# Spreading the gates of a product-key expert layer: one comparison of four tokens against a number row in PSUM

## The chip, the cores and the metric

The kernel runs on one core of a Trainium2 chip. The metric is the device time of one execution in microseconds (us). Five engines matter: TensorE (PE in the profile, its weight loads PEld), VectorE (DVE), ScalarE (ACT), GpSimd (POOL) and SyncE (SP), which here only starts transfers. SBUF is the working memory, PSUM the memory that TensorE writes its products to; each has 128 partitions.

## The reference

Two transformer blocks over 512 tokens of width 1024, in fp32. The first block mixes its tokens by attention and a delta rule, and then passes them through PEER, a layer of 16384 experts with one neuron each. Only PEER's gates are touched here. The second block ends in another expert layer. PEER, cut to what matters:

```
q = x @ w_query                                   # 8 heads, 256 wide
s1, s2 = q[..., :128] @ keys1.T, q[..., 128:] @ keys2.T   # 128 scores each
v1, i1 = top_k(s1, 16);  v2, i2 = top_k(s2, 16)
cand = v1[:, None] + v2[None, :]                  # 256 pairs
top_s, top_p = top_k(cand, 16)
e_idx = i1[top_p // 16] * 128 + i2[top_p % 16]
gate = softmax(top_s)
y = sum over the 8 * 16 chosen: gate * gelu(x . u[e_idx]) * v[e_idx]
```

## The kernel before

Function `peer` computes PEER for the first 384 tokens (ND) without gathering: each meets all 16384 experts, 128 expert tiles of 128, and the gates are zero where an expert wasn't chosen. For the last 128 tokens the chosen rows of u and v are gathered one by one. The steps stand in this order in the code:

- The query projection and the top 16 of each head (`topk`), for all four tiles of 128 tokens.
- `select(tt)`, for each tile of tokens: it turns the places of the chosen pairs into two key numbers, by comparing with a short number row (L1119), multiplying by the key numbers (L1122, on DVE for the first two tiles, on POOL for the others) and adding up (L1123). For the first three tiles the two key numbers and the gate of each choice are transposed and stored as `selT`, with the choices on the partitions and the tokens along the row; `negT` holds two of them negated.
- `spread(tt)`, for the first three tiles: it lays the gates out by expert. A token's 128 gates over i1 and i2 form a 128x128 matrix, the product of two one-hot matrices over the choices: `ohb`, 1 where i2 equals the column's number, and `oha`, the gate where i1 equals it. Four tokens are a group, 32 groups a tile, 96 in all. For each group `onehots` makes `oha` and `ohb`, `product` multiplies them (four matmuls into one PSUM bank, L1169; in fp32 each shows as two passes), `store` copies the bank out (L1175), and every fourth group sends 1 MB of gate columns to DRAM by SP. In program order a group's one-hots stand beside the product of the group before and the store of the one before that. The one-hots have four buffers.
- The 128 columns' numbers 0 to 127 (`k_iota`) lie in SBUF. `MIX` says by tile and parity of the group how a group's four gated one-hots are made: one or none by ACT with two activations (L1160, L1161), one or none by DVE alone in one instruction (L1158), and the other two to four by a comparison on DVE (L1146) that POOL then multiplies by the gates (L1154). `ohb` is one comparison of 512 elements on DVE (L1146).
- `first(et)`, for the first 28 expert tiles, is independent of the gates: the tile of u is split in two parts by ACT and POOL (L170, L171), 24 matmuls give its products with the tokens (L165 to L167, tile `ups`), and ACT takes the gelu (L1007). PE works on these between the products of the spreading.
- After that the expert stage: for each group of eight expert tiles the gates come back from DRAM and are multiplied in (L1275), and v is multiplied in (L165 to L167, tile `vacc`; results added to the residual by L1343), with the remaining `first` tiles and the gathered rows in between.

A planner that walks the program with estimated costs orders the instructions of each engine; dependencies between engines are kept by semaphores, and each engine takes its instructions in that order.

Of the kernel before, what the change touches and what calls it, by code (L numbers as in the profile page):

```python
# [9 lines left out]
F32 = mybir.dt.float32  # L10
# [30 lines left out]
def shape_consts():  # L41
    """Constants that depend on shapes alone."""
# [6 lines left out]
    # attention: distance and log of the number of patterns holding the offset  # L49
# [5 lines left out]
    # delta rule masks: two chunks of 64 on the partitions  # L55
# [31 lines left out]
def layout(I):  # L87
    """Data layout only: transposes, reshapes, concatenation."""
# [49 lines left out]
class K:  # L138
# [34 lines left out]
    def tables(s, after, name="natural_log_exp_and_others"):  # L173
        """one set of tables for what follows an activation, here both of log and exp"""
        with s.tc.issue_after(after.ins):
            s.nc.scalar.preload_act_table_set(name)

    def rsqrt(s, out, x, eps):
        """out = (x + eps) ** -0.5"""
        s.nc.scalar.activation(out, x, AF.Ln, bias=eps)  # L180
        s.nc.scalar.activation(out, out, AF.Exp, scale=-0.5)

    def rsqrt6(s, out, x, tmp, eps=1e-6, bias=None):
        """out = (x + eps) ** -0.5, with a step of Newton's method"""
# [6 lines left out]
    # ---------------------------------------------------------------- modulation  # L191
# [9 lines left out]
    def ada_parts(s, which, wname, bname, rep, lo, n, sel, wp, pp, tags=("mm", "tr"), spaces=None):  # L201
        """mod columns of the n column blocks (512 wide) from lo on, a block to each next(), two row tiles to a load.
        Block q goes to row q of each quarter, a quarter for every fourth row tile; its other rows get zeros."""
# [23 lines left out]
    # ------------------------------------------------- normalised, modulated input  # L227
    def rms(s, xT, wp, pp, tag="mm", ps=None):
        """rsqrt(mean(x*x) + eps)"""
# [12 lines left out]
    def modnorm(s, xT, r, gname, which, part, hhi, hlo, wp, keep=None):  # L242
        """h = x * r * (g * (1 + scale)) + shift, split in two parts."""
# [13 lines left out]
    def proj_tile(s, wsrc, hhi, hlo, wp, pp, eng=None, n=KT, tag="mm"):  # L257
        """One 128-column tile of the first n row tiles of h @ w, columns on partitions; returns the PSUM tile."""
# [11 lines left out]
    def out_proj(s, wname, mhi, mlo, xT, gatecol, wp, pp, ms=None, ahead=None, begun=0):  # L270
        """x += gate * (mix @ w) from tile begun on; the mean of its squares into ms; loads that run ahead of what follows"""
# [20 lines left out]
class Banks:  # L292
    """PSUM banks by tag"""
# [7 lines left out]
def block1(s, alloc, after):  # L301
    nc, tc, A = s.nc, s.tc, s.A
    mm = nc.tensor.matmul
    with ExitStack() as c1:
# [13 lines left out]
        with ExitStack() as c2:  # L318
# [6 lines left out]
            def room():  # L325
                """pools of what runs beside the recurrence"""
# [16 lines left out]
            def tail(forward):  # L343
                """the output projection of all but the last pair beside the last of the recurrence"""
# [24 lines left out]
            with ExitStack() as c3:  # L369
# [13 lines left out]
                # token shift coefficient of the token itself  # L383
# [3 lines left out]
                for ct in [24, 25, 16, 12, 17, 18, 19, 13, 14, 15, 20, 21, 22, 23]:  # L387
# [9 lines left out]
                    if 4 <= j < 8:  # L397
                        # kk: normalised by head
# [45 lines left out]
            # the last pair  # L444
# [23 lines left out]
ATT = 4, 3, 3, 3     # steps of the attention to each filling  # L468
ADA = ((2, 0, 1, 1), (1, 1, 1, 1), (1, 1, 1, 0), (2, 1, 0, 0), (1, 2, 2, 2))    # parts of the modulation to each filling
OUT = 1, 2, 2, 3, 0  # tiles of the output projection to each filling  # L470


def attention(s, P, ap, qkd, vd, mixd):
    """softmax over the three patterns at once, two heads and 128 queries at a time; a step to each next()"""
# [45 lines left out]
def rwkv(s, c, P, zrd, mixd, kkd, sad, gd, room, fill, tail):  # L520
    """Both directions of the delta rule in chunks of 64 steps; the second runs on reversed time.
    Goes on with every next(): constants, gates, the first pair's decays, and the rest, which yields the last
    pair's part of the mix.

    Partitions hold two heads' features (e, f) or two chunks' steps (c, t).  A product that keeps
    the two apart contracts over all 128 partitions, one operand being zero outside its own half.
    """
# [8 lines left out]
    class Room:  # L536
        """a tile in the pool of its tag"""
# [6 lines left out]
    if True:  # L544
        flip = kp.tile([128, 128], F32, name="k_flip")
        # these in places that are needed later
# [8 lines left out]
        ka1 = kp.tile([128, 4], F32, name="ka1")       # 1 - k_a  # L555
# [3 lines left out]
        hwa = kp.tile([128, 16], F32, name="hwa")       # half of w0, a0  # L559
        nc.vector.tensor_scalar(hwa, s.v("w0", 0, 16), 0.5, None, OP.mult)  # L560
        # blocks outside the written ones stay zero
# [22 lines left out]
        def sigmoids(j, dr):  # L584
            """of the decay and of a, 0.5 + 0.5 tanh(x / 2)"""
# [31 lines left out]
        def elementwise(h, dr):  # L617
            """decayed r, kk, b, k of one direction, the last two without their decay"""
# [29 lines left out]
        def by_head(ar, cum, x, y):  # L648
            """b~, k~ of either head"""
# [7 lines left out]
        def within(h, dr, ar, bd, x, y):  # L657
            """products within the chunks"""
            QQ, U, yacc = h.QQ, h.U, h.y
            # token-major  # L660
# [11 lines left out]
            ta = wp.tile([128, 4, 2, 2, 64], F32, name="ta", bufs=3)      # head, (alpha, A_ak v)  # L672
            ps = transposed(ar[:, 0, :])
            nc.scalar.activation(ta[:, :, :, 0, :], ps.rearrange("p a (e f) -> p a e f", e=2), AF.Copy)
            tb = wp.tile([128, 4, 2, 2, 64], F32, name="tb", bufs=3)      # head, (A_rb, b~)
# [5 lines left out]
            # within-chunk products [s, t]  # L681
            db = wp.tile([128, 8, 64], F32, name="db", bufs=1)
            E = wp.tile([128, 8, 64], F32, name="E", bufs=3)
            for t2 in range(2):
                pv = P.tile([128, 2, 2, 2, 64], F32, name="pvy", tag="mm")       # (A_ak v | k~ v y)
                pq = P.tile([128, 2, 2, 64], F32, name="pq", tag="mm")
                for ti in range(2):
                    tt = 2 * t2 + ti
                    pa = P.tile([128, 2, 2, 2, 64], F32, name="pa", tag="mm")     # (b~, k~), head, (alpha, r)
# [27 lines left out]
            # diagonal blocks of 16, one on each lane  # L717
# [8 lines left out]
        def solve(j, dr, held, zd, xd, QQ, PB, RP, y):  # L726
            """(I - A_ab)^-1 and what follows from it"""
            ar, ta, tb, E = held
            Z, V, W = Zb[dr], Vb[dr], Wb[dr]
            # inverses of the blocks of 16, and their transposes for the first three of a chunk  # L730
# [8 lines left out]
            # blocks of 32 from blocks of 16  # L739
# [641 lines left out]
def block2_mix(s, xT, begin_moe, ms=None, pu=None):  # L1381
    nc, tc, A = s.nc, s.tc, s.A
    mm = nc.tensor.matmul
    with ExitStack() as c0:
# [16 lines left out]
        with ExitStack() as c1:  # L1401
# [24 lines left out]
            with ExitStack() as c2:  # L1426
# [122 lines left out]
                def c64(x):  # L1549
                    return x.rearrange("p (c t) -> p c t", t=CH)  # L1550
# [620 lines left out]
```

## Time and profile before

| | |
|---|---|
| median of 3 runs | 2857.38 us |
| lowest and highest | 2854.79 and 2861.47 us |
| span of the profiled execution, first to last instruction | 2856.4 us |
| busy share of the span: PE, DVE, ACT, POOL | 91%, 70%, 37%, 41% |
| selection and spreading | from about 866 to 1145 us |
| busy in it, 893 to 1145: PE, DVE, ACT, POOL | 190, 249, 142, 165 us |

The profile gives no time of its own for its execution beside the span; the median of the runs lies 1.0 us above that. The busy shares of the whole mix stages with different limits, so the stretch of the edit has to be read by itself. Durations of successive instructions on DVE and ACT overlap a little in the trace, so that sums of durations exceed the busy time.

### The profile page before, as it was taken

Reading aid. Unit: us, or ns where it says so; the run is one execution under the profiler, and the core shown is the slowest. Engines: PE = TensorE matmul, PEld = TensorE weight load, DVE = VectorE, ACT = ScalarE, POOL = GpSimd, SP = SyncE. Lnnn points to the kernel's source line nnn. Section 1 sums busy time; section 2 is a strip of 40 time slices with the busy share of each in tenths; the row PEclk is TensorE's granted clock in tenths of the full one; section 3 lists DMA queues with packets and bytes.
Section 4 is the critical chain, followed back from the end, with each engine's and each line's share of the span. In section 5 each row is a group of like instructions: output and inputs, shape, how many; then the busy total and the mean of one; then the engine's idle time right before and its main releaser. Section 6 shows DMA issues by size and latency. Waiting matters only on the chain. (4 is left out here: it accounts for less than half of the span.)

```text
span 2856.4 us, 44680 instructions
## 1 busy us (share of the span) xinstructions
PE 2586.5 (91%) x16918; PEld 2042.6 (72%) x16918; DVE 1999.3 (70%) x3833; ACT 1059.1 (37%) x1946; POOL 1159.9 (41%) x860
## 2 busy tenths in 40 slices
PE   7999888987996786899999999999998999989995
PEld 4764456645886775889999999999986665654442
DVE  3666567544899999788888887878865467563323
ACT  3344434422434465333333333333333353231121
POOL 0012212121534666887776776776542223200002
PEclk9999999998998899999999999999999999889998
DMA  6528763451312465788888888887672222069984
GB/s 243 176 80 273 214 195 87 146 166 58 106 60 76 124 178 166 275 313 312 304 285 282 290 295 286 299 294 270 208 239 96 80 64 79 4 261 413 414 350 170
DMA packets 257160, 587.84 MB, mean 206 GB/s; under 512 B 48024, under 2 KB 120240, under 8 KB 246448
## 3 DMA queue, kind: packets, MB, share of 16 engines
q1 hardware_dynamic: 201856, 393.71, 40.2%
q0 software_dynamic: 38016, 138.43, 14.2%
q10 hardware_dynamic: 17072, 52.83, 5.0%
q8 instruction: 134, 2.20, 0.3%
q14 instruction: 82, 0.67, 0.1%
HBM read 529.05 MB, written 55.84 MB: 205 GB/s over the span
## 5 line engine op out<-in xcount | busy, mean ns | idle before, releaser
L165 PE MATMUL vacc<-gh,vhi 128*128 128x384 f32 x1024 | 346.6, 339 | 19.3 <-DVE xres L1343 13.9
L165 PE MATMUL ups<-phhi,uhi 128*128 128x384 f32 x1024 | 348.8, 341 | 10.4 <-ACT ge L1007 10.4
L167 PE MATMUL ups<-phhi,ulo 128*128 128x384 f32 x1024 | 348.3, 340 | 5.9 <-POOL ulo L171 4.3
L166 PE MATMUL ups<-phlo,uhi 128*128 128x384 f32 x1024 | 348.2, 340 | 1.0 <-DVE phlo L253 1.0
L166 PE MATMUL vacc<-gl,vhi 128*128 128x384 f32 x1024 | 344.8, 337 | 0.7 <-DVE gl L171 0.7
L167 PE MATMUL vacc<-gh,vlo 128*128 128x384 f32 x1024 | 325.6, 339 | 11.2 <-POOL vlo L171 10.2
L170 ACT ACTIVATE vhi<-vraw 128x512 fp32r<-128x512 f32 x256 | 160.2, 631 | 325.1 <-PE vacc L166 130.7
L170 ACT ACTIVATE uhi<-uraw 128x1024 fp32r<-128x1024 f32 x128 | 135.7, 1060 | 302.1 <-PE ups L166 258.7
L1227 DVE CUSTOM_DVE_ANT_0 row<-row,phtok 128x1024 f32<-128x1024 f32 x128 | 203.7, 1594 | 34.2 <-DMA row<-u_rows,peid 28.0
L171 POOL TENSOR_TENSOR vlo<-vraw,vhi 128x512 fp32r<-128x512 f32 x128 | 193.5, 1512 | 78.3 <-ACT vhi L170 71.4
L165 PEld LDWEIGHTS vacc<-gh,vhi 128*128 128x128 f32 x1024 | 194.1, 190 | 25.1 <-DVE xres L1343 18.0
L1232 DVE SCALAR_TENSOR_TENSOR acc<-row,dot,acc 128x1024 f32<-128x1024 f32 x127 | 192.4, 1515 | 19.5 <-DMA row<-peer_v,peid 19.4
L1218 POOL DMA_INDIRECT row<-peer_v,peid x128 | 170.5, 1332 | 86.0 <-DVE acc L1232 36.6
L165 PEld LDWEIGHTS ups<-phhi,uhi 128*128 128x128 f32 x1024 | 196.2, 192 | 10.9 <-ACT ge L1007 10.7
L167 PEld LDWEIGHTS vacc<-gh,vlo 128*128 128x128 f32 x1024 | 191.6, 190 | 15.8 <-POOL vlo L171 12.8
L167 PEld LDWEIGHTS ups<-phhi,ulo 128*128 128x128 f32 x1024 | 195.9, 191 | 7.7 <-POOL ulo L171 5.5
L166 PEld LDWEIGHTS ups<-phlo,uhi 128*128 128x128 f32 x1024 | 196.1, 192 | 1.5 <-DVE phlo L253 1.3
L166 PEld LDWEIGHTS vacc<-gl,vhi 128*128 128x128 f32 x1024 | 194.2, 190 | 1.4 <-DVE gl L171 1.2
L1275 POOL TENSOR_TENSOR ge<-ge,wg 128x384 f32<-128x384 f32 x124 | 162.5, 1319 | 75.2 <-DMA wg<-wdr 60.0
L1218 POOL DMA_INDIRECT row<-u_rows,peid x128 | 171.4, 1339 | 52.5 <-DVE dot L1227 20.5
L171 DVE TENSOR_TENSOR ulo<-uraw,uhi 128x1024 fp32r<-128x1024 f32 x100 | 141.8, 1418 | 45.6 <-ACT uhi L170 45.0
L171 DVE TENSOR_TENSOR vlo<-vraw,vhi 128x512 fp32r<-128x512 f32 x128 | 129.4, 1011 | 52.5 <-ACT vhi L170 50.3
(658 smaller groups left out, 5840.4 us busy)
## 6 DMA issues: line engine op xcount, KB each, us to landing
uraw<-peer_u SPq DMA_DIRECT2D x128, 512.0 KB
vraw<-peer_v SPq DMA_DIRECT2D x256, 256.0 KB
wgu<-w_gu SPq DMA_DIRECT2D x32, 2048.0 KB
adaw<-ada_w SPq DMA_DIRECT2D x96, 512.0 KB
wdn<-w_dn SPq DMA_DIRECT2D x32, 1024.0 KB
wd<-wst SPq DMA_DIRECT2D x20, 1024.0 KB
wg<-wd ACTq DMA_DIRECT2D x16, 1280.0 KB
wraw<-w_in SPq DMA_DIRECT2D x22, 512.0 KB
```

The costliest lines, as they stand in the source:

```text
L165: mm(ps, lhsT=L[0], rhs=R[0], start=first, stop=False)
L166: mm(ps, lhsT=L[0], rhs=R[1], start=False, stop=False)
L167: mm(ps, lhsT=L[1], rhs=R[0], start=False, stop=last)
L170: s.nc.scalar.activation(hi, x, AF.Copy)
L171: return (eng or s.nc.vector).tensor_tensor(lo, x, hi.bitcast(F32), OP.subtract)
L1218: nc.gpsimd.indirect_dma_start(out=r, out_offset=None, in_=(urows, vrows)[which], in_offset=bass.IndirectOffsetOnAxis(ap=eid[:, p:p + 1], ...
L1227: nc.vector.tensor_tensor_reduce(out=r, in0=r, in1=htok, scale=1.0, scalar=0.0, op0=OP.mult, op1=OP.add, accum_out=dot[:, p:p + 1])
L1232: nc.vector.scalar_tensor_tensor(acc, r, dot[:, p:p + 1], acc, OP.mult, OP.add)
L1275: i = (nc.vector if grp == 0 and e % 2 == 0 else nc.gpsimd).tensor_tensor(g3, g3, W[0][:, :, e, :], OP.mult)
```

## The change

It concerns the gated one-hots and the number row. The number row is copied once by ACT into a PSUM bank of its own, and every comparison in `select` and `spread` reads it from there; the bank comes from the transposed tiles (tag `tr`), which go from three buffers to two. The two one-hots of a group become one tile, `oht`, filled by one comparison of 2 x 4 x 128 elements on DVE. The gates are multiplied in afterwards, in place: for two of the four tokens by one POOL instruction, for the other two by one ACT copy each with the gate as scale. `MIX`, `negT` and its activations go. In `select`, the multiply of the second tile of tokens moves from DVE to POOL. The rest of the diff removes comments.

```
-            pp1 = c1.enter_context(tc.tile_pool(name="pq", bufs=3, space=PSUM))
...
+            P = Banks(c1, tc, "pq", mm=3, tr=2, io=1)
...
-            iota = s.const("iota128", kp)
+            iota0 = s.const("iota128", kp)
+            iota = P.tile([128, 128], F32, name="iotap", tag="io")
+            nc.scalar.activation(iota, iota0, AF.Copy)
...
-                    (nc.vector if tt < 2 else nc.gpsimd).tensor_tensor(oh4, oh4, xf[:, :, None, :].to_broadcast([128, 8, 16, 16]), OP.mult)
+                    (nc.gpsimd if tt else nc.vector).tensor_tensor(oh4, oh4, xf[:, :, None, :].to_broadcast([128, 8, 16, 16]), OP.mult)
...
-                nc.scalar.activation(negT[:, :, 128 * tt:128 * tt + 128], ps[:, 0:3:2, :], AF.Copy, scale=-1.0)
...
-                    a = wp.tile([128, 4, 128], F32, name="oha", bufs=4)
-                    b = wp.tile([128, 4, 128], F32, name="ohb", bufs=4)
-                    na, nd = MIX[tt][g % 2]
-                    n = 4 - na - nd                                 # by DVE and Pool; then by DVE alone; then by ACT
-                    if n:
-                        equal(a, 0, n)
-                        nc.gpsimd.tensor_tensor(a[:, 0:n, :], a[:, 0:n, :], selT[:, 2, t0:t0 + n, None].to_broadcast([128, n, 128]), OP.mult)
-                    for i in range(n, 4):
-                        at = slice(t0 + i, t0 + i + 1)
-                        if i < n + nd:
-                            nc.vector.scalar_tensor_tensor(a[:, i, :], iota, selT[:, 0, at], selT[:, 2, at].to_broadcast([128, 128]), OP.is_equal, OP.mult)
-                        else:
-                            nc.scalar.activation(a[:, i, :], iota, AF.Abs, bias=negT[:, 0, at])
-                            nc.scalar.activation(a[:, i, :], a[:, i, :], AF.Relu, scale=negT[:, 1, at], bias=selT[:, 2, at])
-                    equal(b, 1, 4)
-                    made[g] = a, b
+                    o = wp.tile([128, 2, 4, 128], F32, name="oht", bufs=4)
+                    nc.vector.tensor_tensor(o, iota[:, None, None, :].to_broadcast([128, 2, 4, 128]),
+                                            selT[:, 0:2, t0:t0 + 4, None].to_broadcast([128, 2, 4, 128]), OP.is_equal)
+                    nc.gpsimd.tensor_tensor(o[:, 0, 0:2], o[:, 0, 0:2], selT[:, 2, t0:t0 + 2, None].to_broadcast([128, 2, 128]), OP.mult)
+                    for i in range(2, 4):
+                        nc.scalar.activation(o[:, 0, i], o[:, 0, i], AF.Copy, scale=selT[:, 2, t0 + i:t0 + i + 1])
+                    made[g] = o
...
-                        mm(done[g][:, i, :], lhsT=b[:, i, :], rhs=a[:, i, :], start=True, stop=True)
+                        mm(done[g][:, i, :], lhsT=o[:, 1, i], rhs=o[:, 0, i], start=True, stop=True)
```

## Rows read from the trace of the kernel before

**Rows 1.** The page: its span, and PE's busy tenths in 40 equal slices.

```profile
span 2856.4 us, 44680 instructions
...
PE   7999888987996786899999999999998999989995
```

**Rows 2.** Busy time by stretch: stretch, its length, engines' busy time, granted clock, DMA.

```profile
893.00:1020.00 127.00, 99.11 (x589) 94.44 (x588) 126.86 (x143) 64.83 (x135) 80.44 (x51) 0.92 0.37 113
1020.00:1145.00 125.00, 91.27 (x630) 81.69 (x628) 121.89 (x135) 77.56 (x168) 84.17 (x67) 0.99 0.62 180
...
1200.00:1250.00 50.00, 43.37 (x242) 41.77 (x243) 43.15 (x46) 17.78 (x30) 43.44 (x32) 1.00 0.80 289
1250.00:1300.00 50.00, 50.00 (x290) 50.00 (x289) 49.36 (x55) 19.41 (x33) 40.05 (x30) 1.00 0.94 336
```

**Rows 3.** Line groups of DVE, 866 to 1145 us, by shape: count, busy us, mean ns.

```profile
L1146 DVE TENSOR_TENSOR ohb<-k_iota,selT 128x512 f32<-128x512 f32 x96 | 81.2, 846 | 0.0
L1146 DVE TENSOR_TENSOR oha<-k_iota,selT 128x384 f32<-128x384 f32 x48 | 56.5, 1177 | 0.0
L1158 DVE SCALAR_TENSOR_TENSOR oha<-k_iota,selT 128x128 f32<-128x128 f32 x32 | 24.6, 769 | 0.0
L1146 DVE TENSOR_TENSOR oha<-k_iota,selT 128x256 f32<-128x256 f32 x32 | 22.4, 699 | 0.0
L1146 DVE TENSOR_TENSOR oha<-k_iota,selT 128x512 f32<-128x512 f32 x16 | 21.0, 1309 | 0.0
```

**Rows 4.** Timeline of all engines, 1099.7 to 1103.6 us: start, duration, instruction.

```profile
1099.72 1.39 DVE L1146 TENSOR_TENSOR oha<-k_iota,selT 128x384 f32<-128x384 f32 x1
...
1101.04 0.68 DVE L1146 TENSOR_TENSOR ohb<-k_iota,selT 128x512 f32<-128x512 f32 x1
1101.19 1.21 POOL L1154 TENSOR_TENSOR oha<-oha,selT 128x384 f32<-128x384 f32 x1 [0.49 <-DVE oha L1146]
1101.64 1.31 DVE L1146 TENSOR_TENSOR oha<-k_iota,selT 128x512 f32<-128x512 f32 x1
...
1102.45 1.16 PE L1169 MATMUL wps<-oha,ohb 128*128 128x128 f32 x8 [0.54 <-POOL oha L1154]
```

**Rows 5.** Timelines of POOL and DVE from 947 us.

```profile
947.70 4.71 POOL L1122 TENSOR_TENSOR oh<-oh,xf 128x2048 f32<-128x2048 f32 x1 [2.50 <-DVE oh L1119]
...
947.88 4.68 DVE L1158 SCALAR_TENSOR_TENSOR oha<-k_iota,selT 128x128 f32<-128x128 f32 x1
```

**Rows 6.** Instructions of two lines: shortest, median and longest in ns, first and last start.

```profile
L1343 DVE SCALAR_TENSOR_TENSOR xres<-vacc,mod,xres x128: 599/606/619, 1184.0 to 2138.6; 128x384 f32<-128x384 f32 x128
...
L171 DVE TENSOR_TENSOR vlo<-vraw,vhi x128: 675/691/3343, 1151.7 to 2135.8; 128x512 fp32r<-128x512 f32 x128
```

**Rows 7.** A line group of DVE (rsps is in PSUM), and instructions of line 171.

```profile
L1523 DVE TENSOR_TENSOR rst__20857<-rsps,dm 128x512 f32<-128x512 f32 x1 | 0.7, 691 | 0.1
...
L171 DVE TENSOR_TENSOR ulo<-uraw,uhi x100: 1209/1224/2643, 1040.9 to 1991.0; 128x1024 fp32r<-128x1024 f32 x100
```

**Rows 8.** Instructions of lines 1122 and 1154: shortest, median and longest in ns.

```profile
L1122 DVE TENSOR_TENSOR oh<-oh,xf x4: 2278/2282/4480, 873.6 to 924.0; 128x2048 f32<-128x2048 f32 x4
...
L1154 POOL TENSOR_TENSOR oha<-oha,selT x96: 652/1207/1797, 898.1 to 1140.5; 128x384 f32<-128x384 f32 x48, 128x256 f32<-128x256 f32 x32, 128x512 f32<-128x512 f32 x16
```

**Rows 9.** Line groups of ACT, 893 to 1145 us, with its waits behind the second bar.

```profile
L1175 ACT ACTIVATE wst<-wps 128x512 f32<-128x512 f32 x96 | 56.9, 596 | 76.2 <-PE wps L1169 75.0 <-DMA wd<-wst 0.9
L1161 ACT ACTIVATE oha<-oha,selT,negT 128x128 f32<-128x128 f32 x80 | 37.6, 488 | 1.0
L1160 ACT ACTIVATE oha<-k_iota,negT 128x128 f32<-128x128 f32 x80 | 31.2, 394 | 4.2 <-PE wps L1169 4.2
```

**Rows 10.** A line group of PE, 893 to 1145 us, and PE's timeline at 918 us.

```profile
L165 PE MATMUL ups<-phhi,uhi 128*128 128x384 f32 x147 | 52.6, 358 | 0.0
...
918.44 1.05 PE L1169 MATMUL wps<-oha,ohb 128*128 128x128 f32 x8
919.25 0.42 PE L167 MATMUL ups<-phhi,ulo 128*128 128x384 f32 x1
```

More of the change, by code (lines that the diff above doesn't have):

```diff
@@ L804, in rwkv @@
         class Pair:
+            pass
         def begin(j):
@@ L968 @@
 NA = 24
-MIX = (((1, 1), (1, 1)), ((1, 0), (1, 0)), ((1, 0), (0, 0)))
 def peer(s, xT, pu, r, after):
@@ L1012, in peer @@
         with ExitStack() as c1:
-            pp1 = c1.enter_context(tc.tile_pool(name="pq", bufs=3, space=PSUM))
-            class PP:
-                def tile(self, shape, dt, name, tag):
-                    return pp1.tile(shape, dt, name=name, tag=tag)
-            P = PP()
+            P = Banks(c1, tc, "pq", mm=3, tr=2, io=1)
             kp = c1.enter_context(tc.tile_pool(name="pk", bufs=1))
@@ L1028, in peer @@
             selT = kp.tile([128, 3, ND], F32, name="selT")
-            negT = kp.tile([128, 2, ND], F32, name="negT")
             def top16(sets):
@@ L1144, in onehots @@
                     t0 = 128 * tt + 4 * g
-                    def equal(o, which, n):
-                        nc.vector.tensor_tensor(o[:, 0:n, :], iota[:, None, :].to_broadcast([128, n, 128]),
-                                                selT[:, which, t0:t0 + n, None].to_broadcast([128, n, 128]), OP.is_equal)
-                    a = wp.tile([128, 4, 128], F32, name="oha", bufs=4)
-                    b = wp.tile([128, 4, 128], F32, name="ohb", bufs=4)
-                    na, nd = MIX[tt][g % 2]
@@ L1165, in product @@
+                    for i in range(2, 4):
+                        nc.scalar.activation(o[:, 0, i], o[:, 0, i], AF.Copy, scale=selT[:, 2, t0 + i:t0 + i + 1])
+                    made[g] = o
                 def product(g):
-                    a, b = made.pop(g)
+                    o = made.pop(g)
                     done[g] = P.tile([128, 4, 128], F32, name="wps", tag="mm")
                     for i in range(4):
-                        mm(done[g][:, i, :], lhsT=b[:, i, :], rhs=a[:, i, :], start=True, stop=True)
+                        mm(done[g][:, i, :], lhsT=o[:, 1, i], rhs=o[:, 0, i], start=True, stop=True)
@@ L1559, in block2_mix @@
                 class Feat:
+                    pass
                 def prepare(j):
@@ L1670, in block2_mix @@
             class Pair:
+                pass
             def scores(f, pr):
```

## The prediction

> **What bounds the kernel now.** I took the execution of 2856.4 us [rows 1] and asked where the edited code runs. The line groups put every one-hot, gate product and spreading product between about 893 and 1145 us. Then I read the engines stretch by stretch [rows 2]. From 893 to 1145 VectorE (DVE) is busy 126.9 of 127 and 121.9 of 125 us: it sets the pace. TensorE (PE) is busy 99.1 and 91.3 us, so it idles about 62 us here. Right behind, from 1250 on, PE is busy 50.0 of 50 us, and the page's slices, of 71.4 us each, show it at nine tenths or more from the 18th to the 30th, the expert stage [rows 1]. So the time that this stretch loses on PE comes out of the whole, and time taken out of the stretch should pass on to the end, so long as PE has its work earlier.
>
> The line groups of DVE [rows 3] show what it is busy with: five forms of the spreading's one-hots, 205.7 us in 224 instructions. The means don't fit the sizes: 384 elements take 1177 ns, 512 take 846 in one group and 1309 in another. The timeline of a few us in the steady part [rows 4] shows why. The comparison that starts at 1101.64, while the gate multiply on GpSimd (POOL) has run since 1101.19, lasts 1.31 us and ends 0.55 us after POOL's end at 1102.40; the comparison of the same size that starts before POOL at 1101.04 lasts 0.68. It waits for POOL, though no data ties the two. POOL's next multiply needs that comparison, so the two run in turn: the 64 groups of four tokens that fill the stretch from 1020 take about 121.9/64 = 1.90 us each [rows 2]. The clearest case is [rows 5]: a 128x128 one-hot issued 0.18 us into a long POOL multiply takes 4.68 us.
>
> **What the PSUM operand removes.** In the old comparisons both inputs lie in SBUF. Is a DVE instruction with one input in PSUM held up too? [rows 6] compares two lines of the expert stage, in which POOL is as busy: the update that reads a PSUM accumulator and an SBUF tile takes 599 to 619 ns in all 128 instances, while the split with two SBUF inputs goes from 675 up to 3343. So I take the wait as gone for the new comparison. The Trainium skill says the same from the other side (SBUF — State Buffer, section Who interferes with whom): a DVE instruction with at most one SBUF input does not contend with GpSimd, one with two contends with a GpSimd instruction that reads SBUF; by that rule, too, the whole wait goes.
>
> **DVE's price.** The new instruction handles 1024 elements a partition. A two-input instruction with one side in PSUM takes 691 ns for 512, and the unblocked SBUF one of 1024 takes 1209 to 1224 [rows 7], so I take 691 + (1209 - 680) = 1.22 us, 680 being the SBUF form of 512 that nothing holds up [rows 4]. Successive starts overlap by 0.08 us (a 0.68 us instruction at 1101.04, the next at 1101.64 [rows 4]), so a slot is 1.14 us. Then 96 groups cost 109 us. The old ones took 205.7 - 224 x 0.08 = 188 us. Saved: 78 us. Not held up, the old ones would have taken as long as the new: (1209 - 680)/512 = 1.03 ns for each of their 88064 elements and some 0.07 us a slot make 107 us. The edit saves DVE no elements; all of the 78 us are waits for POOL. The bounds of the new instruction: 1.14 us a slot, and, if the wait stays, 1.14 + 0.65 = 1.79.
>
> One page speaks for a dearer operand: the Trainium skill (Perfetto Trace Analysis, section Optimizing Scalar/DVE Operations) gives DVE's access overhead as about 60 ns on SBUF and 125 ns on PSUM. By that the sum would be 96 x 0.065 = 6 us worse; the rows here differ by 11 ns (691 against 680).
>
> **Select.** For the second tile of tokens the masked multiply goes from DVE to POOL: two DVE instructions of 2.28 and 4.48 us, the ends of the line's range [rows 8], so about 6.6 us of slots come off. POOL takes 4.7 us for each [rows 5]; it then sits on the path of that tile's selection, and the small two-SBUF-input steps beside it can be held up as before. Bounds: 0 to -7 us; I take -7. The comparison with the short number row also reads PSUM; it was held up once in eight, 2 us, which I leave out.
>
> **POOL and ACT.** POOL's multiply shrinks from 256 to 512 elements to 256, 0.65 us when alone [rows 8]: 96 x 0.65 = 62 us, hidden beside DVE. ACT drops 80 pairs (31.2 + 37.6 us) and gets 192 copies of 128 elements with a scale from a column. No such row exists: the form with one column as operand takes 0.394 us, with two 0.488 [rows 9], so one with none should take 0.30; I take 0.394, which makes 76 us, with bounds of 58 and 94. ACT's 142 us [rows 2] become about 150, still under DVE. The three negated copies go and one copy of the number row into PSUM comes, long before; together under 1 us. If that cover is gone, ACT's extra 7 us count. The gate columns go out by SP as before, in 24 stores; ACT waits 0.9 us in all for their two buffers [rows 9]. Were each of the 24 waited for as long, it would be 22 us; I count nothing, since groups come closer by less than a third.
>
> **Banks.** The transposed tiles get two buffers instead of three. At worst each of the 16 score tiles waits for an eviction of 0.6 us [rows 9], 10 us; that lies in the top-k, where PE is at nine tenths or more in most slices (the 11th and 12th [rows 1]), so I count nothing and keep the 10 us as a bound.
>
> **PE.** It has 3 x 147 = 441 matmuls of expert tiles left in the stretch, and 96 groups of eight passes of spreading [rows 10]. At full rate an expert matmul takes 50/290 = 0.172 us [rows 2], eight passes take 919.25 - 918.44 = 0.81 us: 76 + 78 = 154 us.
>
> **The sum.** DVE's work from 893 on is 126.9 + 121.9 = 249 us [rows 2]; 249 - 78 - 7 = 164 us if it is never idle. But PE with 154 and ACT with 150 are now next to it, in order, coupled by four buffers of one-hots. Where three engines lie that close, 1200 to 1250, the busiest gets 43.4 of 50 us [rows 2], 0.87. So 164/0.87 = 188 us, a gain of 61. The span 2856.4 becomes 2795; the median of the runs stands 1.0 us above the span, so I forecast 2796 us.
>
> **Rivals.**
> 1. PE gains only where it had run out of expert tiles. Its idle time up to 1020 (28 us [rows 2]) stays; that after 1020 (34 us) goes, all but a few. Gain about 30: 2827. For it: DVE still does all of the selections in order, and products wait on them. Against: from 947 on the long waits for POOL fell on one-hots [rows 5].
> 2. The PSUM operand doesn't end the wait. Then a group costs 1.79 us against 1.90, and 64 x 0.11 + 7 = 14 us come off: 2843. Against it stand the 128 even instances of [rows 6].
> 3. Slower: four buffers become the bound. A buffer is held from the start of its comparison to the end of its product, now 1103.61 - 1099.72 = 3.9 us [rows 4]. If PE works off an expert tile first (24 x 0.172 = 4.1 us) and ACT a split of about 1 us, it is 9 us, 2.25 a group, and 64 x (2.25 - 1.90) = 22 us are lost: 2879. It decides from 7.6 us on. For it: half of each group's gates now hang on ACT, which stands in order behind waits for PE. Against: 441 matmuls are only some 18 expert tiles for 96 groups, and DVE is hardly idle today [rows 2] with four buffers.
> 4. DVE runs nearly full and the held-up small steps get cheaper too: gain 85 to 92, 2765 to 2772.
>
> **Chances.** Forecast (2772 to 2815) 0.68; rival 1 0.15; rival 2 0.06; rival 3 0.06; rival 4 0.05. No more than 2 in 10 is left out between 2768 and 2836. Within 0.2% (5.7 us, about what a measurement of this kernel tells from no change) I put 0.04, from the edge of rivals 2 and 3; slower 0.05, faster 0.91.
>
> **What would show it.** All 96 new comparisons within 1.2 to 1.25 us, none of several us; the last gate copy before about 1090 instead of 1145; ACT copies near 0.39; the expert stage unchanged in length. Wrong it is if comparisons still stretch while POOL runs (rival 2), if DVE waits on products (rival 3), or if the stretch shrinks and PE's full stage doesn't begin earlier.

## The result, and the profile after

The changed kernel takes 2814.35 us (median of 4 runs, 2805.60 to 2820.90), the kernel before on the same chip 2857.99 us: a ratio of 0.9848, with an interval of 0.9823 to 0.9872. That is 43.6 us, where 61 were forecast. The profiled execution has a span of 2819.1 us and so lies 4.8 above the median; single executions of this kernel scatter by some 0.35% to either side.

The page first: its span, and PE's busy tenths by slice, to be read against [rows 1].

```profile
span 2819.1 us, 44546 instructions
...
PE   7999889978997995999999999999979999989995
```

The three engines' instructions on the new tile `oht` (count, then shortest, median and longest in ns, first and last start in us) answer to [rows 3], [rows 8] and [rows 9].

```profile
L1143 ACT ACTIVATE oht<-oht,selT x192: 384/395/420, 907.5 to 1081.3; 128x128 f32<-128x128 f32 x192
L1139 DVE TENSOR_TENSOR oht<-iotap,selT x96: 1208/1216/1226, 906.3 to 1077.3; 128x1024 f32<-128x1024 f32 x96
L1141 POOL TENSOR_TENSOR oht<-oht,selT x96: 602/612/1524, 911.0 to 1078.6; 128x256 f32<-128x256 f32 x96
```

All 96 comparisons lie within 18 ns of each other, and POOL runs beside them. In [rows 3] means didn't fit the sizes; here no comparison is held up while it runs.

Busy time by stretch, columns as in [rows 2]:

```profile
893.00:1020.00 127.00, 117.53 (x795) 114.95 (x793) 103.65 (x94) 82.55 (x187) 84.21 (x71) 0.97 0.56 170
1020.00:1085.00 65.00, 54.95 (x397) 52.63 (x395) 56.35 (x48) 52.80 (x141) 33.03 (x45) 0.95 0.80 230
1085.00:1145.00 60.00, 33.47 (x164) 33.15 (x164) 42.81 (x39) 13.32 (x25) 46.11 (x38) 0.74 0.70 247
1145.00:1200.00 55.00, 54.06 (x305) 52.50 (x305) 47.63 (x57) 21.50 (x37) 45.02 (x35) 1.00 0.80 278
1250.00:1300.00 50.00, 50.00 (x289) 49.94 (x290) 39.98 (x46) 19.08 (x31) 37.52 (x28) 1.00 0.86 299
```

Up to 1020 DVE no longer sets the pace (103.65 of 127, before 126.86) and PE gets 117.53 us instead of 99.11. The spreading is over by 1085. But then, from 1085 to 1145, PE is busy for 33.47 of 60 us at a granted clock of 0.74, the weakest of these stretches. That is the place to look at. Three marks of the hand-over, as instructions (times as above): the end of the last tile's selection, the copies of the last gates, and the products of the expert stage.

```profile
L1123 DVE SCALAR_TENSOR_TENSOR peid<-selp x1: 649/649/649, 1101.0 to 1101.0; 128x128 int32<-128x128 f32 x1
...
L1164 ACT ACTIVATE wg<-wst x4: 294/300/310, 1066.6 to 1083.0; 128x128 f32<-128x128 f32 x4
...
L165 PE MATMUL vacc<-gh,vhi x1024: 333/334/689, 1112.1 to 2101.0; 128*128 128x384 f32 x171
```

In the kernel before, the same three:

```profile
L1130 DVE SCALAR_TENSOR_TENSOR peid<-selp x1: 2484/2484/2484, 1018.2 to 1018.2; 128x128 int32<-128x128 f32 x1
...
L1183 ACT ACTIVATE wg<-wst x4: 309/310/311, 1121.3 to 1143.8; 128x128 f32<-128x128 f32 x4
...
L165 PE MATMUL vacc<-gh,vhi x1024: 333/334/689, 1147.5 to 2137.9; 128*128 128x384 f32 x171
```

The last gate copy is 60.8 us earlier, the first expert product only 35.4. The expert stage itself lasts as long as before (1112.1 to 2101.0, 988.9 us, against 990.4). In between, the timeline shows (start, duration, instruction, idle time before it and what ended that):

```profile
1077.25 1.23 DVE L1139 TENSOR_TENSOR oht<-iotap,selT 128x1024 f32<-128x1024 f32 x1 [2.06 <-PE wps L1150]
...
1078.39 2.28 DVE L1112 TENSOR_TENSOR oh<-ab,iotap 128x2048 f32<-128x2048 f32 x1
...
1082.98 0.31 ACT L1164 ACTIVATE wg<-wst 128x128 f32<-128x128 f32 x1
...
1098.65 2.29 DVE L1116 TENSOR_REDUCE selp<-oh 128x128 f32<-128x2048 f32 x1 [4.67 <-POOL oh L1115]
1100.97 0.65 DVE L1123 SCALAR_TENSOR_TENSOR peid<-selp 128x128 int32<-128x128 f32 x1
1101.72 3.83 ACT L170 ACTIVATE gh<-ge 128x384 fp32r<-128x384 f32 x9 [18.43 <-DVE peid L1123]
...
1105.97 0.69 PE L165 MATMUL ups<-phhi,uhi 128*128 128x384 f32 x1 [23.66 <-ACT ge L1004]
```

The planner has put the last tile's selection behind the last comparison of the spreading. ACT's first split of the gated tiles (`gh`) waits 18.4 us for the end of that selection, a gelu (`ge`) stands behind it on ACT, and PE waits 23.7 us for the gelu. No data tie `gh` to `peid`; the pool of `gh` opens in the code where the selection's pools have closed.

### The profile page after: what moved, and what is told of

Read it like the earlier page. It is cut to its first block, busy times and chain, and to the rows that moved or that the text cites. A ratio compares the mean times of both kernels' runs of the same rounds, so it can differ in the third digit from the quotient of the medians.

```text
span 2819.1 us, 44546 instructions
## 1 busy us (share of the span) xinstructions
PE 2574.9 (91%) x16918; PEld 2042.7 (72%) x16918; DVE 1912.5 (68%) x3703; ACT 1054.9 (37%) x1976; POOL 1111.0 (39%) x862
## 5 line engine op out<-in xcount | busy, mean ns | idle before, releaser
L1256 POOL TENSOR_TENSOR ge<-ge,wg 128x384 f32<-128x384 f32 x124 | 150.8, 1223 | 74.5 <-DMA wg<-wdr 57.3
```

The source lines that it names most:

```text
L1256: i = (nc.vector if grp == 0 and e % 2 == 0 else nc.gpsimd).tensor_tensor(g3, g3, W[0][:, :, e, :], OP.mult)
```

## The experiments

The table puts the marks side by side (start times from each profile, in us). "Matmuls" are PE's records from 866 to 1300 us, a measure of how far PE has come at a fixed time; some records can be missing from a trace. At full rate one is worth 0.172 us. Each ratio is to the kernel before on the same chip.

| kernel | last selection | last gate copy | first product | matmuls | median us | ratio, interval |
|---|---|---|---|---|---|---|
| before | 1018.2 | 1143.8 | 1147.5 | 2073 | 2857.99 | 1 |
| changed | 1101.0 | 1083.0 | 1112.1 | 2308 | 2814.35 | 0.9848, 0.9823 to 0.9872 |
| e2, row in SBUF | 1008.1 | 1137.4 | 1140.3 | 2084 | 2858.18 | 1.0014, 0.9994 to 1.0034 |
| e3, row in PSUM alone | 1124.9 | 1104.8 | 1136.3 | 2171 | 2844.59 | 0.9970, 0.9944 to 0.9997 |
| e8, e3 with an earlier selection | 1030.8 | 1128.4 | 1132.0 | 2181 | 2838.79 | 0.9944, 0.9913 to 0.9975 |
| e4, multiply back on DVE | 1107.1 | 1089.3 | 1118.4 | 2311 | 2814.83 | 0.9852, 0.9818 to 0.9885 |
| e1, select(3) before spread(2) | 1058.9 | 1097.3 | 1101.3 | 2290 | 2817.95 | 0.9861, 0.9825 to 0.9897 |
| e5, select(3) before spread(1) | 1020.2 | 1095.6 | 1100.1 | 2331 | 2807.02 | 0.9820, 0.9795 to 0.9845 |
| e6, all selections first | 961.5 | 1093.0 | 1097.7 | 2383 | 2808.99 | 0.9833, 0.9805 to 0.9862 |
| e7, select(3) by DVE alone | 1093.7 | 1079.8 | 1105.2 | 2343 | 2819.95 | 0.9868, 0.9841 to 0.9896 |
| e11, changed again | 1101.9 | 1083.3 | 1112.1 | 2306 | 2816.44 | 0.9851, 0.9819 to 0.9883 |
| e9, gh in its own memory | 1101.6 | 1079.0 | 1111.0 | 2317 | 2812.73 | 0.9862, 0.9829 to 0.9895 |
| e12, e9 with e5's order | 1016.9 | 1092.9 | 1097.6 | 2332 | 2814.38 | 0.9849, 0.9820 to 0.9879 |
| e10, five buffers | 1094.3 | 1078.1 | 1105.6 | 2361 | 2797.46 | 0.9784, 0.9754 to 0.9815 |

### e2: the whole change, but the number row stays in SBUF

```
-            iota = P.tile([128, 128], F32, name="iotap", tag="io")
-            nc.scalar.activation(iota, iota0, AF.Copy)
+            iota = iota0
```

> The changed kernel with the number row left in SBUF, everything else as changed. Theory: the whole gain is the wait for POOL that the PSUM operand removes; the 1024-element comparisons should stretch from 1.22 to 1.8 us and more (several up to 5 us behind POOL's long multiplies), the last gate copy should come at 1130 to 1150 us, and the time should be 2840 to 2860. Rival: the gain comes from the joined comparison and from POOL's shorter multiply, and the operand is of no account; then comparisons stay near 1.22 us and the time near 2814.

2858.18 us: the whole gain is gone. The same comparison, on the same tile, with only the row's place changed:

```profile
L1138 DVE TENSOR_TENSOR oht<-k_iota,selT x96: 1210/1629/5626, 906.0 to 1132.5; 128x1024 f32<-128x1024 f32 x96
L1140 POOL TENSOR_TENSOR oht<-oht,selT x96: 602/1588/2596, 907.3 to 1134.6; 128x256 f32<-128x256 f32 x96
```

The shortest is as short as with PSUM (1210 against 1208 ns), the median 413 ns longer and the longest 4.4 us longer. POOL's multiply, too, goes from a median of 612 to 1588. So DVE and POOL hold each other up, and the PSUM operand ends it for the comparisons and for most of POOL's multiplies. The regrouping without the row brings nothing: the interval runs from 0.9994 to 1.0034.

### e3 and e8: the row in PSUM, the old groups kept

e3 is the kernel before with the edit of the number row and of the banks alone; `MIX`, `oha` and `ohb` stay.

```
-            iota = s.const("iota128", kp)
+            P = Banks(c1, tc, "pq", mm=3, tr=2, io=1)
...
+            iota0 = s.const("iota128", kp)
+            iota = P.tile([128, 128], F32, name="iotap", tag="io")
+            nc.scalar.activation(iota, iota0, AF.Copy)
```

> The kernel before with the number row in PSUM and nothing else of the change (the banks of its transposed tiles reduced as in the change). Theory: the one-hots fall to their unblocked durations (0.42 us for 256, 0.56 for 384, 0.70 for 512 elements, 0.35 for the small form), DVE's 78 us are saved by this line alone, the last gate copy comes at 1080 to 1100 us and the time is 2805 to 2830. Rival: without the regrouping POOL's long multiplies (1.2 us for 512 elements) pace the groups and no more than half is gained: 2830 to 2850.

2844.59 us, a ratio of 0.9970: the rival's figure, not mine, though the waits do not show its cause, POOL's long multiplies. DVE is freed: its 96 comparisons for `ohb` take 677 to 693 ns (in the kernel before up to 2884), its one-instruction one-hots 338 to 346 ([rows 5] had one of 4.68 us). But the groups don't follow. Waits from 893 to 1150 us (engine and line waiting, for whom: us in all, times, longest):

```profile
POOL oha L1151 <- DVE oha L1143: 78.6, 68, 5.9
DVE ohb L1143 <- ACT oha L1157: 43.8, 72, 2.2
```

DVE now waits 72 times for ACT's one-hots, the two activations that the old mix gives to one token in 80 of the 96 groups, and POOL for DVE. The last gate copy starts at 1104.8, not at 1083. Part of this is a tie that e3 itself makes, as a group in its steady part shows (timeline):

```profile
1049.46 0.55 DVE L1143 TENSOR_TENSOR oha<-iotap,selT 128x384 f32<-128x384 f32 x1
...
1050.04 0.37 ACT L1157 ACTIVATE oha<-iotap,negT 128x128 f32<-128x128 f32 x1 [0.18 <-DVE oha L1143]
...
1050.44 0.69 DVE L1143 TENSOR_TENSOR ohb<-iotap,selT 128x512 f32<-128x512 f32 x1 [0.43 <-ACT oha L1157]
1050.44 0.49 ACT L1158 ACTIVATE oha<-oha,selT,negT 128x128 f32<-128x128 f32 x1
1050.85 0.60 ACT L1172 ACTIVATE wst<-wps 128x512 f32<-128x512 f32 x1
1051.05 0.55 DVE L1143 TENSOR_TENSOR oha<-iotap,selT 128x384 f32<-128x384 f32 x1
```

The comparison for `ohb` uses nothing that ACT's activation makes; all that the two share is the row in PSUM, which in e3 both engines read. DVE, ACT and DVE read it in turn, and a group takes 1.59 us. In all, that activation waits 32.8 us for DVE in e3; in the kernel before, with the row in SBUF, it waits only for PE [rows 9]. ACT's own three instructions fill 1.41 of the 1.59 us (1050.04 to 1051.45), so ACT would come next even without this tie. A variant in which ACT keeps reading the row from SBUF was not run, so how much of the missing gain is the tie and how much the old groups is not shown.

e8 gives e3 the order of e5 (below), to see whether only the late selection, 1124.9 here, holds e3 back.

```
-            for tt in range(4):
-                if tt == 3:
-                    spread(2)
-                select(tt)
-                if 0 < tt < 3:
-                    spread(tt - 1)
+            for f, tt in ((select, 0), (select, 1), (spread, 0), (select, 2), (select, 3), (spread, 1), (spread, 2)):
+                f(tt)
```

> The kernel before with the number row in PSUM alone and the selection of the last tile written before the spreading of the second tile. Theory: the row alone frees DVE, and what hid it in the run with the row alone was that the late selection held up the expert stage (31 us from the last gate copy to the first product). Then the last gate copy stays near 1105 us or earlier, the first product follows within 6 us, and the time falls to 2815 to 2830. Rival: the two activations by ACT for a quarter of the tokens and POOL's long multiplies bound the groups, and the earlier start is taken up later: 2838 to 2848 as with the row alone.

2838.79 us, within the rival's bounds, and not told apart from e3 by the intervals. In this form, with ACT reading the same bank, the row alone is worth 0.3 to 0.6 per cent, the regrouping alone nothing, both together one and a half.

### e4: the second tile's multiply back on DVE

```
-                    (nc.gpsimd if tt else nc.vector).tensor_tensor(oh4, oh4, ...)
+                    (nc.vector if tt < 2 else nc.gpsimd).tensor_tensor(oh4, oh4, ...)
```

> The changed kernel with the masked multiply of the second tile of tokens back on DVE. My sum took 7 us for its move to POOL. If that held, this run would be 5 to 8 us slower than the changed kernel, 2820 or so. In the trace after, the move made three small steps of DVE wait 4.6, 2.3 and 2.4 us behind POOL's multiply, so the rival is that the move brought nothing: 2808 to 2818.

The ratio is 0.9852 against 0.9848: the medians show nothing of the move, which I had put at -7 us. Their intervals, 7 to 10 us to either side, could not show 7. The marks say a little more. By the last gate copy the changed kernel is 6.3 us ahead of e4, but 2.9 of these it has already ahead of the edited selection (the reciprocal in the first tile's selection starts at 868.28 against 871.17), so some 3.4 us of the 7 arrive there at most. The changed kernel's timeline shows where the rest went:

```profile
891.58 4.57 DVE L1104 TENSOR_TENSOR ab<-ab,cf 128x128 f32<-128x128 f32 x1
```

That small step of the next selection reads two SBUF operands and stands beside POOL's long multiply; two more behind it, beside POOL's splits of u, take 2.31 and 2.36 us, where such steps take about 0.28 elsewhere. Much of what DVE no longer multiplies it waits.

### e1, e5 and e6: the last selection written earlier

Theory: the late selection opens the gap at the hand-over; written earlier, it closes it. e1 writes `select(3)` ahead of `spread(2)`, e5 ahead of `spread(1)` (diff under e8), e6 all four selections ahead of all spreading.

```
             for tt in range(4):
-                if tt == 3:
-                    spread(2)
                 select(tt)
-                if 0 < tt < 3:
+                if 0 < tt:
                     spread(tt - 1)
```

> The changed kernel, with the selection of the last tile of tokens written ahead of the spreading of the third tile. Theory: in the changed kernel ACT's first split of the expert stage waits 18 us for the last instruction of that selection (peid, 1101.6 us), and PE stands idle 23.7 us behind it; that is why the expert stage starts only 35 us earlier although the last gate copy is 61 us earlier. With the selection earlier the first expert product should follow the last gate copy within some 5 us and the time should fall by 15 to 24 us, to 2790 to 2800. Rival: the expert stage starts late for want of something else (v tiles, gates read back, buffers freed by the spreading itself); then the idle stretch of PE stays and the time stays at 2806 to 2821.

The gap does close: the first product follows the last gate copy after 4.0 us instead of 29.1. But the time is 2817.95 us, no gain. PE's time is lost earlier: it stands for 14.4 us up to 1057.2, for gate multiplies that POOL reaches only behind the selection's two long ones (4.5 us each), and the spreading ends 14 us later. The stretch in e1 (columns as in [rows 2]):

```profile
1040.00:1060.00 20.00, 5.19 (x30) 4.80 (x30) 15.01 (x11) 6.53 (x17) 12.04 (x8) 0.70 0.43 126
```

In the changed kernel PE is busy for 17.85 of these 20 us.

> The changed kernel with the selection of the last tile written before the spreading of the second tile, so that it falls where PE still has expert tiles to work off. Theory after the run before: wherever that selection stands once PE has run out of expert tiles, it costs PE some 15 to 24 us, since DVE stands in order behind POOL's two multiplies; here it should cost PE little. The last gate copy should come at 1080 to 1090 us, the first expert product within 6 us of it, and the time should be 2795 to 2808 against 2814 for the changed kernel. Rival: the first 100 us of the expert stage have a bound of their own (v tiles, splits, the first gates), so that starting them earlier only stretches them; then the time stays at 2810 to 2820, with the matmuls done by 1300 us near 2318.

> The changed kernel with all four selections ahead of any spreading. Theory: PE works off expert tiles meanwhile (18 left, 4.1 us each) and the spreading then runs without a stop; the last gate copy comes at 1080 to 1095 us and the time is 2795 to 2812. Rival: PE runs out of tiles that it may hold before the spreading begins, idles in the selections by 15 us or more, and the time is 2815 to 2830.

Here the selection lies where PE still has expert tiles to work on. PE comes further by 1300 us (2331 and 2383 matmuls against 2308), and the medians are 2807.02 and 2808.99. But DVE now does the selection within the spreading, and the last gate copy comes at 1095.6 and 1093.0 (for e5, 1080 to 1090 was expected). By the ratios the gains over the changed kernel are some 8 and 4 us; the intervals overlap with its own, so a gain is shown for neither.

### e7: the last selection made shorter

```
-                    (nc.gpsimd if tt else nc.vector).tensor_tensor(oh4, oh4, ...)
+                    (nc.gpsimd if 0 < tt < 3 else nc.vector).tensor_tensor(oh4, oh4, ...)
```

> The changed kernel with the last tile's two masked multiplies on DVE (2.3 us each) instead of POOL (4.5 us each), the order as in the changed kernel. If the wait at the start of the expert stage is the length of that last selection, the gap between the last gate copy and the first expert product falls from 29 us to about 15 to 20. Theory: the time falls by some 5 to 10 us, to 2804 to 2810. Rival, that the first 100 us of the expert stage take up any earlier start: 2811 to 2820.

The gap from the last gate copy to the first product goes from 29.1 to 25.4 us, where 15 to 20 were expected; the time of 2819.95 us shows nothing of it.

### e11, e9 and e12: is it memory that ties gh to the selection?

e11 is the changed kernel unaltered, as the measure for the next three.

> The changed kernel once more, unaltered, as the measure for the three kernels run beside it. Both theories expect 2808 to 2822 us and a ratio to the kernel before near 0.985.

2816.44 us, as expected. e9 takes two of the nine buffers of `gh` and `gl` from a pool that is open from the start, so that the first two lie where no tile of the selection lay; the order in the code and the number of buffers stay.

```
+        gp0 = c0.enter_context(tc.tile_pool(name="pg0", bufs=LEAD))
         with ExitStack() as c1:
...
-            gp = c1.enter_context(tc.tile_pool(name="pg", bufs=9))
+            gp = c1.enter_context(tc.tile_pool(name="pg", bufs=7))
...
-                gh = gp.tile([128, ND], F32R, name="gh")
-                gl = gp.tile([128, ND], F32R, name="gl")
+                gh = (gp0 if et % 9 < 2 else gp).tile([128, ND], F32R, name="gh")
+                gl = (gp0 if et % 9 < 2 else gp).tile([128, ND], F32R, name="gl")
```

> The changed kernel with two of the nine gh and gl buffers in memory that the selection never used; order of the code, work and number of buffers as in the changed kernel. Theory: ACT's first gh waits 18.4 us for the last selection because its tile lies where the selection's tiles lay. Then that wait is gone, the first expert product starts before 1100 us instead of 1112, though the last selection ends as late as before, and 8 to 20 us come off the changed kernel run beside it. Rival: the wait goes and the first product comes earlier, but the first 100 us of the expert stage are paced by the splits of v, and the time stays within 5 us of the changed kernel's. Another rival: the wait stays, since something other than memory ties gh to the selection.

The tie was memory: the selection ends as late as ever, and `gh` starts 19 us ahead of that. Timeline of e9:

```profile
1082.05 0.52 ACT L170 ACTIVATE gh<-ge 128x384 fp32r<-128x384 f32 x1 [2.72 <-DVE ge L1257]
...
1087.65 0.69 PE L165 MATMUL ups<-phhi,uhi 128*128 128x384 f32 x1 [9.30 <-ACT ge L1004]
...
1101.56 1.07 DVE L1124 SCALAR_TENSOR_TENSOR peid<-selp 128x128 int32<-128x128 f32 x1
```

PE is back at 1087.65 instead of 1105.97. But only two of the nine buffers are untied. The third `gh` comes from the old pool and waits for `peid` as before, a gelu stands behind it on ACT, and PE stands for another 7.9 us (timeline of ACT, then of PE):

```profile
1102.73 3.00 ACT L170 ACTIVATE gh<-ge 128x384 fp32r<-128x384 f32 x7 [3.54 <-DVE peid L1124]
...
1106.16 0.69 PE L165 MATMUL ups<-phhi,uhi 128*128 128x384 f32 x1 [7.88 <-ACT ge L1004]
```

So the first product starts at 1111.0 all the same, also because PE does expert tiles of u first: before its first product it has 1372 matmul records from 866 us on, the changed kernel 1326, so this start understates e9 by some 46 x 0.172 = 8 us. From 1085 to 1145 us e9 does 54 matmuls more than e11 (218 against 164), and from 1145 to 1200 it does 52 fewer (247 against 299). PE's waits in e9 from 1145 to 1200 us show one that takes them:

```profile
PE vacc L165 <- DVE xres L1325: 9.0, 1, 9.0
```

PE stands for the accumulators, which DVE has not yet added to the residual. The time is 2812.73 us, 3.7 below e11, inside what scatter gives: the theory was right on the wait, and its price of 8 to 20 us did not show, with the tie cut for the first two tiles and not for the others.

e12 is e9 with e5's order.

> The order of e5 (last tile's selection ahead of the second spreading) and the gh buffers in their own memory. If the late selection costs time only by gh's wait, this is no faster than own memory alone, within 4 us. If the place of the selection matters for itself (DVE's work moved to where PE still has expert tiles), it is 4 to 10 us faster than own memory alone, 2795 to 2805.

2814.38 us: the earlier selection adds nothing to own memory. Of these six variants (e1, e5, e6, e7, e9, e12) none has an interval clear of the changed kernel's; in e1 and e9 the traces show the loss moved to another place.

### e10: five buffers of one-hots

```
-                    o = wp.tile([128, 2, 4, 128], F32, name="oht", bufs=4)
+                    o = wp.tile([128, 2, 4, 128], F32, name="oht", bufs=5)
```

> The changed kernel with five buffers of one-hots instead of four. Theory: four were enough, DVE waited only 15 us in all for products to free a buffer; the time stays within 5 us of the changed kernel's, and the last gate copy stays within 5 us of 1083. The prediction's third rival: the buffers pace the groups; then 8 to 15 us come off.

My theory fell. 2797.46 us, 19.0 below e11 on the same chip, more also than the 8 to 15 of the rival, and the intervals (0.9754 to 0.9815, 0.9819 to 0.9883) do not meet. Timeline of DVE at the end of the spreading, first e11 with four buffers, then e10 with five:

```profile
1064.34 10.27 DVE L1139 TENSOR_TENSOR oht<-iotap,selT 128x1024 f32<-128x1024 f32 x9 [0.48 <-PE wps L1150]
1078.13 1.23 DVE L1139 TENSOR_TENSOR oht<-iotap,selT 128x1024 f32<-128x1024 f32 x1 [3.52 <-PE wps L1150]
1079.28 2.28 DVE L1112 TENSOR_TENSOR oh<-ab,iotap 128x2048 f32<-128x2048 f32 x1
...
1101.86 0.65 DVE L1123 SCALAR_TENSOR_TENSOR peid<-selp 128x128 int32<-128x128 f32 x1
```

```profile
1059.09 10.27 DVE L1139 TENSOR_TENSOR oht<-iotap,selT 128x1024 f32<-128x1024 f32 x9
1069.28 2.28 DVE L1112 TENSOR_TENSOR oh<-ab,iotap 128x2048 f32<-128x2048 f32 x1
1078.47 4.36 DVE L1256 TENSOR_TENSOR ge<-ge,wg 128x384 f32<-128x384 f32 x4 [6.92 <-ACT wg L1164]
...
1094.34 0.65 DVE L1123 SCALAR_TENSOR_TENSOR peid<-selp 128x128 int32<-128x128 f32 x1
```

With four, DVE waits for products to free a buffer (17.5 us in 22 waits from 893 to 1085, the last of them 3.5 us), and the selection queued behind its last comparison starts at 1079.28. With five (12.6 us in 8) DVE has run ahead, the selection starts 10.0 us earlier and ends 7.5 earlier, and the first product comes 6.5 us earlier. The expert stage behind it is 6.1 us shorter (977.4 against 983.5), and what follows it 2.6 us, which together is the 15.2 us between the two profiled spans. The planner's order differs between the two kernels as well, and the two profiled executions of the changed kernel alone differ by 5.4 us in that stage, so only the 6.5 us at the hand-over is traced to the buffer; the rest stays open.

## Why the prediction was right in its mechanism and too large by 18 us

**The range.** The measured 2814.35 us lies 0.65 us inside the forecast range of 2772 to 2815, and the same kernel in e11 took 2816.44. That the range held is luck; the size was too large.

**The wait for POOL goes.** Right. Forecast 1.22 us a comparison, measured 1.208 to 1.226, none held up; e2 shows that the row's place alone does it. The rule cited from the Trainium skill (SBUF — State Buffer, section Who interferes with whom) is borne out: 96 of 96 with one SBUF input run free, 96 with two go up to 5626 ns. By the figures of the Trainium skill's other page (Perfetto Trace Analysis, section Optimizing Scalar/DVE Operations) each would be dearer by an estimated 65 ns; the shortest with PSUM and with SBUF differ by 2 ns (1208 and 1210), so here the measurement decides.

**DVE's 78 us as a gain of the row.** Half right. The forecast read them as waits for POOL, and they were; my expectation of e3 concluded that the row alone would bring most of the gain. e3 brought 0.3% and e8 0.6%: with the old mix the groups are then paced by DVE and ACT in turn, in part because both read the row's bank. In the changed kernel ACT no longer reads the row, its pair of activations is one copy (384 to 420 ns, forecast 394) and POOL's share is smaller (median 612 ns, forecast 652). Which of these lets the freed time be used was not taken apart.

**Select, -7 us.** Not borne out: at most some 3.4 us arrive at the last gate copy, and the time shows nothing, though it could not exclude 7. Much of the work that came off DVE came back as held-up small steps with two SBUF operands, the risk that the prediction named and set at the good end.

**The stretch, 188 us at 0.87.** From 893 to the last gate copy at 1083.0 it is 190 us; the copy came 60.8 us earlier, forecast 61, and the mark set for it was 1090. But this agreement is in good part luck. The forecast's 164 us of DVE work contain the last tile's selection, and the planner put that selection's long DVE instructions (four of some 2.3 us each) behind the stretch; what is left, 158.3 us, fills 0.83 of the 190. Where the selection is done inside, as in the kernel before, the copy comes at 1095.6 (e5), 1093.0 (e6) and 1092.9 (e12), 200 to 203 us after 893, with DVE busy for 171.4, 169.0 and 171.5 us of them. So DVE's work was forecast 5 to 7.5 us too small and its share a little too high (0.87, where it is 0.85 to 0.86): like for like the stretch was forecast 12 to 15 us too short, give or take the few us by which these traces differ in where the spreading begins.

**"Time taken out of the stretch should pass on to the end, so long as PE has its work earlier."** This is the step that was too large. Of 60.8 us, 35.4 arrive at the first product; as PE has done 20 more matmuls by then (1326 against 1306), it is about 39 at equal work. The condition behind "so long as" failed at a place I had not read: the last tile's selection, which in the kernel before ends at 1018.2 in the middle of the spreading, was planned behind it, and `gh` takes its memory. e9 shows the tie. e1, e5 and e12, in which the gap is closed, show that closing it does not bring back its 23.7 us of idle PE: their intervals exclude so large a gain. What is closed there opens behind POOL's multiplies (e1) or at the accumulators (e9).

**The buffers.** Rival 3 was put as a loss, and no loss came. But its mechanism costs within the gain: a fifth buffer gives 19.0 us, and with it stands, at 2797.46, what was forecast for four, 2796. I had read from DVE's nearly full busy time with four buffers [rows 2] that they were enough; that time was itself waits for POOL, so it said nothing of a DVE that no longer waits.

**The rest.** Rival 1 (only the idle time after 1020 goes) is refuted by PE's 117.53 of 127 us up to 1020; rival 2 by the comparisons; rival 4 by DVE's 158.3 busy us of 190 and by the small steps that are still held up. Why e10's expert stage is shorter, and which place bounds the first 100 us of it once the gap is closed, stays open.

## What to carry to other kernels

Where two engines hold each other up, moving a constant operand to the other memory can free both for the price of a PSUM bank; but look for the partner that paces the chain next, and for a second engine that reads the same bank, since the row alone gave a fifth to two fifths of what row and regrouping gave together. And look at what the forecast counts inside a stage. One that ends 61 us earlier hands over only as early as the last thing queued behind it: look up what the planner put there, and which finished tiles' memory the next stage takes. A buffer count that was enough for a stalled engine has to be tried anew once the stall is gone.

## What the runs showed of the hardware that was not expected

A gap on PE costs more than its length. In e9, after 9.3 us of idle time, PE's matmuls start 0.32 us apart; a few us later they are 0.18 apart. Timeline of PE in e9:

```profile
1088.14 0.52 PE L166 MATMUL ups<-phlo,uhi 128*128 128x384 f32 x1
...
1088.46 0.52 PE L167 MATMUL ups<-phhi,ulo 128*128 128x384 f32 x1
...
1092.56 0.33 PE L166 MATMUL ups<-phlo,uhi 128*128 128x384 f32 x1
...
1092.74 0.33 PE L167 MATMUL ups<-phhi,ulo 128*128 128x384 f32 x1
```

The granted clock is 0.51 from 1087.6 to 1092.2 us and 1.00 from 1092.5 to 1096: the level of 1.2 GHz, then that of 2.4. The 14 matmuls that start in the first of these stretches take 4.57 us, where 14 x 0.172 = 2.41 would do at full rate, so the gap of 9.3 us cost some 2.2 more. The changed kernel shows the same behind its gap of 23.7 us: a granted clock of 0.50 from 1105.9 to 1111, 1.00 from 1111.2 to 1115. And the wait between DVE and POOL runs both ways: with the row in SBUF, POOL's multiply of 256 elements had a median of 1588 ns, with the row in PSUM 612.
